# Sixteen of 22 FFN inner tiles from 2x2 block problems, four blocks run into each other, and a key block moved behind a product of the mixer

## The chip, the cores and the metric

One core of a Trainium2 chip runs the whole program: TensorE (PE in the profile), its weight loader (PEld), VectorE (DVE), ScalarE (ACT), GpSimd (POOL) and SyncE (SP), and 16 DMA engines that serve two queues here, a hardware queue fed by SP and a software queue fed by POOL. The metric is the device time of one execution in microseconds, the median of three runs. The kernel before takes 1901.01 us.

## The reference

Two layers, each a token mixer of three branches and a SwiGLU FFN, on 512 rows of 1024 columns, all in float32. What the change touches is the FFN, and in the mixer only an order.

```python
D_MODEL = 1024; SEQ = 512; DEPTH = 2
FFN_HIDDEN = -(-8 * D_MODEL // (3 * 256)) * 256          # 2816, 22 tiles of 128
...
for l in range(DEPTH):
    h = jnp.einsum('bsd,de->bse', x, w_in[l])
    rq, rk, rv, rg, cq, ck, cv, dq, dk, dv, gates = jnp.split(h, splits, axis=-1)
    ...
    x = _layer_norm(DEEPNORM_ALPHA * x + mix, ln1_g[l], ln1_b[l])
    u = jnp.einsum('bsd,df->bsf', x, w_ffn_in[l])
    u_gate, u_up = jnp.split(u, 2, axis=-1)
    ffn = jnp.einsum('bsf,fd->bsd', jax.nn.silu(u_gate) * u_up, w_ffn_out[l])
    x = _layer_norm(DEEPNORM_ALPHA * x + ffn, ln2_g[l], ln2_b[l])
```

## The kernel before

**Arithmetic.** Every float32 operand is held as a pair of float32r values, hi and lo, and a product of two pairs is three matmuls (`mm3`, L122 to L124: hi by hi, lo by hi, hi by lo). A weight block of 128 x 2048 values arrives by DMA in a staging buffer `st` (four of them). ACT casts it to `wh` (L259, or L154 in two pieces of 1024) and DVE subtracts to `wl` (L260, or L155). There are three buffers each of `wh` and `wl`, in rotation: the fourth block from here reuses the buffer of the first, and its cast waits until PE has read that one for the last time. A DVE subtraction waits for the cast of its block.

**Plain tiles.** `u_ffn(i)` makes inner tile i of the FFN: gate and up columns, 8 row blocks, three matmuls each of 128x512, so 48 matmuls into two `pt` banks, then tanh, products and the split into the pair `hid`.

**Block problems.** A 2x2 block problem replaces 8 block products by 7, after Strassen and Winograd. For the FFN's first matrix `u_fin(pb)` makes four inner tiles (gate and up) at once, as seven products called m1, y, m2, v, x, g and h, of 24 matmuls each: 168 matmuls of 128x512 into `pf` banks where four plain tiles take 192. The seven weight operands are sums of four 1 MiB blocks of the matrix. Class `Chain` makes them with four loads by SP (L174) and four accumulating DMAs by POOL (L178, `accum_op=ALU.add`): one staging buffer `a` is loaded for m1, and after each split the next block is added onto it for y, x and h; m2 and v load blocks of their own; g takes a buffer `c` that was filled ahead. An accumulating DMA onto `a` can start only when ACT and DVE have read `a`. Class `Close`, so far used only in the mixer, has five loads and two accumulating DMAs, `a` and `c`, both ahead of their use, and two additions of 128x2048 on DVE (L233, L239) for the other two sums. The seven results are summed on DVE and ACT into natural order (rows by inner columns), where tanh and the products are applied (`gate_half`, `gated`); `s_turn` brings them back by 128x128 transposes on PE into `ph` banks (L1241), eight per call and two calls per block, and ACT copies them out as halves `hf` (L1243).

**Second matrix.** The FFN's output is made in two groups of eight inner tiles by block problems (`fout_items`, o for tiles 0 to 7 and w for 8 to 15, both `Chain`) and a plain rest (tiles 16 to 21, `fout_rest`). The hidden operand of o comes from blocks p and q as `Twins`, whose sums run over halves of 128x512; that of w comes from plain tiles 8 to 15 as `Quarters` (`s_hid`, sums of 128x256 columns, L292 to L295). The first product of o also issues the eight loads of the residual `z` (L455); DVE adds the products to `z` (L1302 the first time, L1304 after).

**Order.** Two lists written by hand, one for the mixer and one for the FFN, give the order of items; an item has its weights, its PE work and two groups of side steps that run within it. Weights are asked for up to three items ahead. A scheduler then moves single instructions of each engine a little. Each engine, SP and POOL work through their instructions strictly in order. In the mixer the two blocks p and q (retention values and gates) are run beside each other's neighbours, and `u_rqk(rk, RK, 1)`, the second key block, stands between q's products m1 and y.

Of the kernel before, what the change touches and what calls it, by code (L numbers as in the profile page):

```python
# [13 lines left out]
F32R = mybir.dt.float32r  # L14
# [14 lines left out]
FFN = 2816  # L29
# [23 lines left out]
REST = 16  # L53
# [3 lines left out]
def trunk(ctx, tc, x_in, xT_in, w_in, ret_norm_g, da_norm_g, lq1, lk1, lq2, lk2, w_a, w_b, w_c, b_merge, w_out,  # L57
# [19 lines left out]
    def g(dt=F32, name="g"):  # L77
        return gp.tile([P, 512], dt, tag="g", name=name)
# [183 lines left out]
    class Quarters:  # L262
# [15 lines left out]

        def parts(self, t1, t2, scale):

            q, p2 = g(F32R, "q11"), Pair("q2")
            part_hi(q[:, self.A], t1[:, self.A], scale)
            part_lo(q[:, self.B], t1[:, self.A], q[:, self.A], scale)
            split(p2, t2, scale=scale)
            self.use["m1"] = q[:, self.A], q[:, self.B]
            self.put("m2", p2, self.A)
            self.put("h", p2, self.B)

        def sums(self, t1, t2, scale=None):
# [12 lines left out]
    class Twins:  # L302
# [33 lines left out]

# [271 lines left out]
    def layer(l):  # L608
# [506 lines left out]
        for (specs, fn), *groups in [  # L1115
# [3 lines left out]
            (p["x"], [q["a"]]), (u_rqk(rq, RQ, 1),), (p["g"], [q["c"]]), (p["h"],),  # L1119
            (q["m1"], [], [s_r2(0)]), (u_rqk(rk, RK, 1), [s_r2(1)], [s_r3(0)]), (q["y"], [], [s_r3(1)]),  # L1120
            (q["v"], [s_dh(2)]), (q["m2"], [], [s_r1(2)]), (q["x"], [s_dh(3)]), (u_cqk(0), [], [s_r1(3)]), (q["g"],), (q["h"],),
            (u_gate(2, 0), [s_r2(2)], [s_r2(3), s_r3(2)]), (u_cqk(1), [s_r3(3)] + c(0)[0], c(0)[1]),
# [72 lines left out]
        def ffn_done(i, pg, pu):  # L1195
            t = g(name="fth")
            nc.scalar.activation(t, pg, AF.Tanh, scale=0.5)
            nc.vector.scalar_tensor_tensor(t, t, 1.0, pg, op0=ALU.add, op1=ALU.mult)
            nc.vector.tensor_mul(t, t, pu)  # L1199
            if i >= REST:  # L1200
                hid[i] = Pair("hid")
                split(hid[i], t, scale=0.5)
            else:
                hid[i] = t

        def s_hid(k):

            def fn():
                r0, kh = GROUPS[1]
                t1, t2 = hid[r0 + k], hid[r0 + kh + k]  # L1210
                hid[r0 + k], hid[r0 + kh + k] = Quarters(), None
                hid[r0 + k].parts(t1, t2, 0.5)
                hid[r0 + k].sums(t1, t2, 0.5)
            return fn

# [31 lines left out]

        def s_ready(fp):
            def fn():
                twins[fp] = Twins(half.pop((0, 0, fp)), half.pop((0, 1, fp)))  # L1250
                twins[fp].ready(half.pop((1, 0, fp)))
                hid[2 * fp], hid[2 * fp + 1] = twins[fp].each
            return fn

        def s_twins(fp):
            def fn():
                twins.pop(fp).sums(half.pop((1, 1, fp)))
            return fn
# [108 lines left out]

        p, q, o, w = u_fin(0), u_fin(1), fout_items(0), fout_items(1)
        for (specs, fn), *groups in [
            (u_ffn_first([8, 9]), [s_natural(0)], [s_x1(0)]), (u_ffn(10), [s_x1(1), s_x1(2)], [s_x1(3), s_natural(1)]),  # L1370
            (p["m1"], [s_natural(2)], [p["c"], s_natural(3)]), (u_ffn(11),), (p["y"],), (p["m2"],),
            (p["v"],), (p["x"],), (u_ffn(12), [], [s_turn(0, 0)]), (p["g"],), (p["h"],),
            (q["m1"], [], [q["c"]]), (u_ffn(13), [s_turn(0, 1)]), (q["y"],), (q["m2"],),
            (q["v"],), (q["x"],), (u_ffn(14), [], [s_turn(1, 0)]), (q["g"],), (q["h"], [s_ready(0)], [s_ready(1)]),
            (o["m1"], [], [s_turn(1, 1)]), (u_ffn(15), [s_twins(0)], [s_twins(1), o["c"]]), (o["m2"],), (o["y"],), (u_ffn(16),),
            (o["v"],), (o["x"],), (u_ffn(17),), (o["g"], [], [s_hid(0)]), (o["h"], [], [s_hid(1)]), (u_ffn(18), [s_hid(2)], [s_hid(3)]),
            (w["m1"],), (u_ffn(19), [], [w["c"]]), (w["m2"],), (w["y"],), (u_ffn(20),),
            (w["v"],), (w["x"],), (u_ffn(21),), (w["g"],), (w["h"],),
        ]:
            item(specs, fn, *groups)  # L1380
# [61 lines left out]
```

## Time and profile before

| | |
|---|---|
| median of three runs | 1901.01 us (1900.52 to 1903.43) |
| profiled execution, its own time | 1905.45 us |
| its span | 1903.7 us, mean granted TensorE clock 0.997 |
| PE busy | 1886.1 us, 99% |
| weight loads (PEld) | 1588.1 us, 83% |
| DVE | 1290.6 us, 68% |
| ACT | 931.2 us, 49% |
| DMA, hardware queue | 237.01 MB, 38.4% of 16 engines' span |
| DMA, software queue (accumulating) | 46.56 MB, 14.5% |

PE is busy nearly all the time, so the time is the length of PE's own work plus the few stretches in which it waits. The recorded duration of a matmul is longer than its pace, because successive matmuls overlap; the pace is read from a stretch of PE time divided by the matmuls in it. The FFN of the first layer lies at 603 to 915 us of the span, that of the second at 1550 to 1861 us. Durations of DVE, ACT and DMA instructions can be read from the groups directly.

### The profile page before, as it was taken

To read this page: it belongs to the slowest core of one execution; us is meant where nothing else is said; L and a number is where in the kernel's file an instruction comes from. 1 tells how busy PE (TensorE), PEld (TensorE's weight loads), DVE (VectorE), ACT (ScalarE), POOL (GpSimd) and SP (SyncE) were. 2 spreads that over 40 slices of the span, in tenths; PEclk is the share of its full clock that TensorE was granted. 3 is DMA by queue.
4 is the path that set the end of the run, shared out by engine and by line. 5 is a ranking of instruction groups with operands and counts; after the bars stand their busy time and mean duration, and the time that the engine had idled before them with its cause. 6 is when DMAs were issued, how large, how long until landed. Compare 5 with 4: busy or idle time off the path is not lost. (4 is left out here: it accounts for less than half of the span.)

```text
span 1903.7 us, 24003 instructions
## 1 busy us (share of the span) xinstructions
PE 1886.1 (99%) x9170; PEld 1588.1 (83%) x9170; DVE 1290.6 (68%) x2047; ACT 931.2 (49%) x1547; POOL 114.0 (6%) x141
## 2 busy tenths in 40 slices
PE   9999999999999999999999999999999999999998
PEld 7888788888888888888898887888888888888886
DVE  6776766667766855775677767566776668467756
ACT  5545555567634444443355545545765344344430
POOL 2000000000000010000010000000000000000000
PEclk9999999999999999999999999999999999999999
DMA  9595344332155577766375844533322546876561
GB/s 282 151 285 150 119 141 128 111 119 81 56 173 160 154 172 179 202 155 155 111 201 171 273 111 122 171 108 109 122 67 77 189 121 165 189 181 185 144 154 44
DMA packets 239346, 285.09 MB, mean 150 GB/s; under 512 B 8580, under 2 KB 147936, under 8 KB 239232
## 3 DMA queue, kind: packets, MB, share of 16 engines
q1 hardware_dynamic: 215232, 237.01, 38.4%
q0 software_dynamic: 24000, 46.56, 14.5%
q8 instruction: 72, 1.18, 0.3%
q14 instruction: 42, 0.34, 0.1%
HBM read 260.42 MB, written 23.12 MB: 149 GB/s over the span
## 5 line engine op out<-in xcount | busy, mean ns | idle before, releaser
L122 PE MATMUL pt<-xTh,wh 128*128 128x512 f32 (+1 forms) x1328 | 498.3, 376 | 0.9 <-ACT wh L154 0.8
L124 PE MATMUL pt<-xTh,wl 128*128 128x512 f32 (+1 forms) x1328 | 494.4, 373 | 0.0
L123 PE MATMUL pt<-xTl,wh 128*128 128x512 f32 (+1 forms) x1328 | 494.3, 372 | 0.0
L155 DVE TENSOR_TENSOR wl<-st,wh 128x1024 fp32r<-128x1024 f32 (+1 forms) x236 | 257.2, 1113 | 102.0 <-ACT wh L154 87.4
L154 ACT CAST wh<-st 128x1024 fp32r<-128x1024 f32 (+1 forms) x236 | 220.2, 961 | 210.8 <-PE pt L123 84.4
L260 DVE TENSOR_TENSOR wl<-st,wh 128x2048 fp32r<-128x2048 f32 x98 | 224.6, 2292 | 122.1 <-ACT wh L259 121.1
L124 PEld LDWEIGHTS pt<-xTh,wl 128*128 128x128 f32 x1328 | 250.6, 189 | 43.9
L122 PEld LDWEIGHTS pt<-xTh,wh 128*128 128x128 f32 x1328 | 250.5, 189 | 43.3 <-ACT wh L154 1.5
L123 PEld LDWEIGHTS pt<-xTl,wh 128*128 128x128 f32 x1328 | 251.1, 189 | 41.8
L259 ACT CAST wh<-st 128x2048 fp32r<-128x2048 f32 x98 | 187.3, 1912 | 173.8 <-PE pt L123 73.9
L122 PE MATMUL pf<-wh,xTh 128*128 128x512 f32 x240 | 94.0, 392 | 0.4 <-ACT rph L106 0.4
L123 PE MATMUL pf<-wl,xTh 128*128 128x512 f32 x240 | 93.9, 391 | 0.0
L124 PE MATMUL pf<-wh,xTl 128*128 128x512 f32 x240 | 93.5, 390 | 0.0
L123 PE MATMUL pf<-wl,s12h 128*128 128x512 f32 x192 | 75.9, 395 | 3.2 <-DVE wl L260 3.2
L122 PE MATMUL pf<-wh,s12h 128*128 128x512 f32 x192 | 75.6, 395 | 2.2 <-ACT wh L259 2.2
L122 PE MATMUL pf<-wh,s43h 128*128 128x512 f32 x192 | 75.8, 395 | 0.0
L124 PE MATMUL pf<-wh,s12l 128*128 128x512 f32 x192 | 75.3, 393 | 0.0
L123 PE MATMUL pf<-wl,s43h 128*128 128x512 f32 x192 | 75.3, 392 | 0.0
L124 PE MATMUL pf<-wh,s43l 128*128 128x512 f32 x192 | 75.1, 391 | 0.0
L383 ACT COPY sw<-pt 32x512 f32<-32x512 f32 (+1 forms) x96 | 55.6, 579 | 33.0 <-PE pt L124 31.8
L1199 DVE TENSOR_TENSOR fth<-fth,pt 128x512 f32<-128x512 f32 x28 | 19.2, 687 | 68.7 <-PE pt L124 68.4
L750 ACT COPY tc<-pf 128x512 f32<-128x512 f32 x60 | 34.1, 586 | 54.2 <-PE pf L124 53.0
(341 smaller groups left out, 3494.4 us busy)
## 6 DMA issues: line engine op xcount, KB each, us to landing
st<-in_w_in SPq DMA_DIRECT2D x60, 1024.0 KB, 5.2
st<-in_w_ffn_in SPq DMA_DIRECT2D x56, 512.0 KB, 5.6
st<-in_w_ffn_out SPq DMA_DIRECT2D x20, 1024.0 KB, 5.1
st<-in_w_in SPq DMA_DIRECT2D x32, 512.0 KB, 5.1
st<-in_w_ffn_in SPq DMA_DIRECT2D x16, 1024.0 KB, 5.8
st<-in_w_ffn_in POOLq DMA_DIRECT2D x16, 1024.0 KB, 9.4
st<-in_w_ffn_out POOLq DMA_DIRECT2D x16, 1024.0 KB, 8.6
st<-in_w_in POOLq DMA_DIRECT2D x12, 1024.0 KB, 11.1
```

The costliest lines, as they stand in the source:

```text
L122: nc.tensor.matmul(ps, lh, rh, start=start, stop=False, skip_group_check=onto)
L123: nc.tensor.matmul(ps, lh, rl, start=False, stop=False, skip_group_check=onto)
L124: nc.tensor.matmul(ps, ll, rh, start=False, stop=stop, skip_group_check=onto)
L154: return [nc.scalar.copy(self.hi[:, a:b], self.st[:, a:b]), nc.vector.tensor_sub(self.lo[:, a:b], self.st[:, a:b], f(self.hi[:, a:b]))]
L155: nc.vector.tensor_sub(self.lo[:, a:b], self.st[:, a:b], f(self.hi[:, a:b]))]
L259: nc.scalar.copy(self.hi, st)
L260: nc.vector.tensor_sub(self.lo, st, f(self.hi))
L383: nc.scalar.copy(sw[half * b:half * b + half], ps[half * o:half * o + half])
L750: nc.scalar.copy(t[to, j], ps)
L1199: nc.vector.tensor_mul(t, t, pu)
```

## The change

In each layer's FFN, inner tiles 0 to 15 come from four block problems p, q, r, u (`Chain`, `Close`, `Chain`, `Close`); six plain tiles, 16 to 21, are left. Both output groups take their hidden operands from halves by `Twins`, whose sums are cut in three (`difference`, `sums`, `rest`) so that each can be placed by itself; `Quarters.parts` and `s_hid` go. A block's m1 stands ahead of the last two products of the block before it, and the first products of the output group o stand inside u. In the mixer's list q's y stands ahead of the second key block instead of behind it.

```diff
         def ready(self, a12):
             self.a12 = a12
             self.part("m1", self.a11)
             self.part("m2", a12)
-        def sums(self, a22):
-            t = g(name="ta")
-            nc.vector.tensor_sub(t, self.a21, a22)
-            self.part("y", t)
+        def difference(self, a22):
+            self.a22, self.t = a22, g(name="ta")
+            nc.vector.tensor_sub(self.t, self.a21, a22)
+            self.part("y", self.t)
+        def sums(self):
+            t = self.t
             nc.vector.tensor_sub(t, t, self.a11)
             self.part("x", t)
             nc.vector.tensor_add(self.a12, self.a12, t)
             self.part("v", self.a12)
+        def rest(self):
             nc.vector.tensor_sub(self.a21, self.a11, self.a21)
             self.part("g", self.a21)
-            self.part("h", a22)
+            self.part("h", self.a22)
...
-            (q["m1"], [], [s_r2(0)]), (u_rqk(rk, RK, 1), [s_r2(1)], [s_r3(0)]), (q["y"], [], [s_r3(1)]),
-            (q["v"], [s_dh(2)]), (q["m2"], [], [s_r1(2)]), ...
+            (q["m1"], [], [s_r2(0)]), (q["y"], [s_r2(1)]), (u_rqk(rk, RK, 1), [], [s_r3(0)]),
+            (q["v"], [s_dh(2)], [s_r3(1)]), (q["m2"], [], [s_r1(2)]), ...
...
-        def u_fin(pb):
-            return u_two(Chain(w_ffn_in[l], 0, 4, (512 * pb, FFN + 512 * pb)), x1q,
+        def u_fin(pb, kind):
+            return u_two(kind(w_ffn_in[l], 0, 4, (512 * pb, FFN + 512 * pb)), x1q,
                          functools.partial(gate_half, pb), functools.partial(gated, pb))
...
-        p, q, o, w = u_fin(0), u_fin(1), fout_items(0), fout_items(1)
+        p, q, r, u = u_fin(0, Chain), u_fin(1, Close), u_fin(2, Chain), u_fin(3, Close)
+        o, w = fout_items(0), fout_items(1)
         for (specs, fn), *groups in [
-            (u_ffn_first([8, 9]), [s_natural(0)], [s_x1(0)]), (u_ffn(10), [s_x1(1), s_x1(2)], [s_x1(3), s_natural(1)]),
-            (p["m1"], [s_natural(2)], [p["c"], s_natural(3)]), (u_ffn(11),), (p["y"],), (p["m2"],),
-            (p["v"],), (p["x"],), (u_ffn(12), [], [s_turn(0, 0)]), (p["g"],), (p["h"],),
-            (q["m1"], [], [q["c"]]), (u_ffn(13), [s_turn(0, 1)]), (q["y"],), (q["m2"],),
-            (q["v"],), (q["x"],), (u_ffn(14), [], [s_turn(1, 0)]), (q["g"],), (q["h"], [s_ready(0)], [s_ready(1)]),
-            (o["m1"], [], [s_turn(1, 1)]), (u_ffn(15), [s_twins(0)], [s_twins(1), o["c"]]), (o["m2"],), (o["y"],), (u_ffn(16),),
-            (o["v"],), (o["x"],), (u_ffn(17),), (o["g"], [], [s_hid(0)]), (o["h"], [], [s_hid(1)]), (u_ffn(18), [s_hid(2)], [s_hid(3)]),
-            (w["m1"],), (u_ffn(19), [], [w["c"]]), (w["m2"],), (w["y"],), (u_ffn(20),),
-            (w["v"],), (w["x"],), (u_ffn(21),), (w["g"],), (w["h"],),
+            (u_ffn_first([16, 17]), [s_natural(0)], [s_x1(0)]), (p["m1"], [s_x1(1)], [s_x1(2)]),
+            (u_ffn(18), [s_x1(3), s_natural(1)], [p["c"]]), (p["m2"], [s_natural(2)], [s_natural(3)]), (p["y"],),
+            (p["v"], [q["a"]]), (u_ffn(19),), (p["x"],), (q["m1"],), (p["g"], [s_turn(0, 0)]), (p["h"],),
+            (q["y"], [q["c"]]), (q["v"], [s_turn(0, 1)]), (q["m2"],), (q["x"],), (r["m1"],), (q["g"], [s_turn(1, 0)]), (q["h"],),
+            (r["y"],), (r["m2"], [s_turn(1, 1)], [r["c"]]), (r["v"], [u["a"]]), (r["x"],), (u["m1"],), (r["g"], [s_turn(2, 0)]),
+            (r["h"], [s_ready(0, 0)], [s_ready(0, 1)]),
+            (u["y"], [u["c"]]), (u["v"], [s_turn(2, 1)]), (u["m2"],), (u["x"],),
+            (o["m1"], [s_differ(0, 0)], [s_differ(0, 1)]), (u["g"], [s_turn(3, 0)]), (u["h"], [s_sums(0, 0)], [s_sums(0, 1)]),
+            (o["m2"],), (o["y"], [s_turn(3, 1)], [o["c"]]), (u_ffn(20), [s_rest(0, 0)], [s_rest(0, 1)]), (o["v"], [s_ready(1, 0)], [s_ready(1, 1)]),
+            (o["x"],), (w["m1"], [s_differ(1, 0)], [s_differ(1, 1)]), (o["g"],), (o["h"], [s_sums(1, 0)], [s_sums(1, 1)]),
+            (w["m2"], [s_rest(1, 0)], [s_rest(1, 1)]), (w["y"], [w["c"]]), (u_ffn(21),), (w["v"],), (w["x"],),
+            (w["g"],), (w["h"],),
```

How this moves instructions is shown at three places of the first layer. The second layer has the same order.

In the mixer, on PE, around q's product x. Before, `wh_1431` is the operand of q's y, `wh_1713` that of q's x, and the two share a buffer; `prt` are transposes of another step.

```order
L122 MATMUL pf_1680<-wh_1431,s12h_616 128x512
L123 MATMUL pf_1680<-wl_1432,s12h_616 128x512
L124 MATMUL pf_1680<-wh_1431,s12l_617 128x512
L853 MATMUL prt_1695<-ident_75,ro_1598 128x128 x2
L853 MATMUL prt_1695<-ident_75,ro_1601 128x128 x2
L853 MATMUL prt_1704<-ident_75,ro_1598 128x128 x2
L853 MATMUL prt_1704<-ident_75,ro_1601 128x128 x2
L122 MATMUL pf_1435<-wh_1713,s12h_472 128x512
```

After, `wh_1695` is the operand of q's x; it shares its buffer with the key block's weights. PE reads those for the last time ahead of eight transposes and the 24 matmuls of q's v (operand `wh_1515`), of which the last three are the first rows here.

```order
L122 MATMUL pf_1583<-wh_1515,s43h_618 128x512
L123 MATMUL pf_1583<-wl_1516,s43h_618 128x512
L124 MATMUL pf_1583<-wh_1515,s43l_619 128x512
L848 MATMUL prt_1729<-ident_75,ro_1577 128x128 x2
L848 MATMUL prt_1729<-ident_75,ro_1580 128x128 x2
L848 MATMUL prt_1738<-ident_75,ro_1577 128x128 x2
L848 MATMUL prt_1738<-ident_75,ro_1580 128x128 x2
L122 MATMUL pf_1435<-wh_1695,s12h_472 128x512
```

Between the last reader of the shared buffer and q's x stood eight transposes; now the whole of v and sixteen transposes stand there.

On POOL, from the last row tiles of the LayerNorm ahead of the FFN (`rs`, a power) to the end of block problems. Before:

```order
L494 TENSOR_TENSOR rs_5331<-rs_5331,mhalf_83 128x1
L494 TENSOR_TENSOR rs_5425<-rs_5425,mhalf_83 128x1
L178 DMA st_5854<-in_w_ffn_in 128x4x512
L178 DMA st_5695<-in_w_ffn_in 128x4x512 x3
L178 DMA st_6248<-in_w_ffn_in 128x4x512
L178 DMA st_6139<-in_w_ffn_in 128x4x512 x3
L178 DMA st_6804<-in_w_ffn_out 128x4x512
L178 DMA st_6541<-in_w_ffn_out 128x4x512 x3
```

After (up to the first accumulation for the second output group):

```order
L489 TENSOR_TENSOR rs_5331<-rs_5331,mhalf_83 128x1
L178 DMA st_5430<-in_w_ffn_in 128x4x512
L489 TENSOR_TENSOR rs_5425<-rs_5425,mhalf_83 128x1
L178 DMA st_5857<-in_w_ffn_in 128x4x512
L178 DMA st_5430<-in_w_ffn_in 128x4x512
L178 DMA st_5970<-in_w_ffn_in 128x4x512
L178 DMA st_5430<-in_w_ffn_in 128x4x512
L178 DMA st_6222<-in_w_ffn_in 128x4x512
L178 DMA st_6286<-in_w_ffn_in 128x4x512
L178 DMA st_6565<-in_w_ffn_in 128x4x512
L178 DMA st_6286<-in_w_ffn_in 128x4x512
L178 DMA st_6588<-in_w_ffn_in 128x4x512
```

The first accumulation now stands ahead of the last `rs`, and accumulations of one block's chain (`st_5430` is p's, `st_6286` is r's) alternate with those for the next block's `a` and `c`.

On DVE, from the first product of o to its second. Before, `wl_6634` and `wl_6696` are splits, the rows L1302 add o's m1 to `z`, and then come the sums of `Twins`.

```order
L260 TENSOR_TENSOR wl_6634<-st_6631,wh_6633 128x2048
L112 TENSOR_TENSOR qm2l_6628<-hf_6539,qm2h_6627 128x512
L260 TENSOR_TENSOR wl_6696<-st_6541,wh_6695 128x2048
L1302 TENSOR_SCALAR z_6637<-z_6637,pf_6653 128x512
L1302 TENSOR_SCALAR z_6639<-z_6639,pf_6667 128x512
L327 TENSOR_TENSOR ta_6754<-hf_6316,hf_6686 128x512
```

After, the same additions (L1295) stand between the last sums of block u and `wl_6992`, the split of o's m2.

```order
L260 TENSOR_TENSOR wl_6930<-st_6770,wh_6929 128x2048
L1211 TENSOR_TENSOR tc12_6854<-fth_6894,tc12_6854 128x512
L1295 TENSOR_SCALAR z_6933<-z_6933,pf_6949 128x512
L1295 TENSOR_SCALAR z_6935<-z_6935,pf_6963 128x512
L317 TENSOR_TENSOR ta_6977<-hf_6263,hf_6539 128x512
L260 TENSOR_TENSOR wl_6992<-st_6989,wh_6991 128x2048
```

The split that PE needs next thus stands behind additions that need the loads of `z`, which on SP come behind the load of that split's own block:

```order
L174 DMA st_6989<-in_w_ffn_out 128x4x512
L450 DMA z_6933<-saved0_80 128x512
L150 DMA st_7092<-in_w_ffn_in 128x8x128
L450 DMA z_6934<-saved0_80 128x512
L450 DMA z_6935<-saved0_80 128x512
L450 DMA z_6936<-saved0_80 128x512
```

Before, the eight loads of `z` (L455) stood in one piece behind the two loads of a plain tile's weights, and the next split behind the additions was that of plain tile 15, not of a product of o.

More of the change, by code (lines that the diff above doesn't have):

```diff
@@ L277, in put @@
             self.use[name] = pr.hi[:, sl], pr.lo[:, sl]
[L279 to L287, printed above, removed]
         def sums(self, t1, t2, scale=None):
@@ L1199, in ffn_done @@
             nc.vector.tensor_mul(t, t, pu)
[L1200 to L1214, printed above, removed]
+            hid[i] = Pair("hid")
+            split(hid[i], t, scale=0.5)
         nat, half = {}, {}
@@ L1246, in layer, with s_ready, s_differ, s_sums @@
         twins = {}
[L1248 removed]
+        def s_ready(gi, fp):
             def fn():
[L1250 to L1252 removed]
+                pa, pc, k = 2 * gi, 2 * gi + 1, 8 * gi + 2 * fp
+                tw = twins[gi, fp] = Twins(half.pop((pa, 0, fp)), half.pop((pa, 1, fp)))
+                tw.ready(half.pop((pc, 0, fp)))
+                hid[k], hid[k + 1] = tw.each
             return fn
[L1255 removed]
+        def s_differ(gi, fp):
             def fn():
[L1257 removed]
+                twins[gi, fp].difference(half.pop((2 * gi + 1, 1, fp)))
+            return fn
+        def s_sums(gi, fp):
+            def fn():
+                twins[gi, fp].sums()
+            return fn
+        def s_rest(gi, fp):
+            def fn():
+                twins.pop((gi, fp)).rest()
             return fn
```

2 lines of the change are left out of this document (1 added, 1 removed).

## The prediction

> **What bounds the kernel now.** I read the head of the profile page first, then the waits of PE, then the FFN in stretches, then the DMA queues.
>
> ```profile
> span 1903.7 us, 24003 instructions
> PE 1886.1 (99%) x9170; PEld 1588.1 (83%) x9170; DVE 1290.6 (68%) x2047; ACT 931.2 (49%) x1547; POOL 114.0 (6%) x141
> ```
>
> ```profile
> PE pf L123 <- DVE wl L260: 3.2, 2, 1.6
> PE pf L122 <- ACT wh L259: 2.2, 2, 1.1
> PE warm L579 <- POOL ident masks.py:199: 1.5, 1, 1.5
> PE pt L122 <- ACT wh L154: 0.8, 1, 0.8
> ```
>
> PE is the bound, and its listed waits (us in total, times, longest) are a few microseconds in the whole program. So a change is worth the PE work it removes, less the waits it makes. Two thirds of the waits are one pair of rows, twice each; the first pair lies here:
>
> ```profile
> PE pf L123 <- DVE wl L260: 1.6, 1, 1.6
> PE pf L122 <- ACT wh L259: 1.1, 1, 1.1
> ```
>
> That is the answer for 190 to 205 us, and it is q's product x in the mixer: its cast waits until y has left the shared buffer, and only eight transposes of PE work cover it. The same pair stands in layer two.
>
> The first layer's FFN, in stretches (columns: length, then busy time and count of PE, PEld, DVE, ACT, POOL, then clock, DMA share, GB/s):
>
> ```profile
> 603.00:915.00 312.00, 311.71 (x1489) 262.12 (x1488) 208.09 (x259) 135.72 (x167) 21.17 (x17) 1.00 0.69 171
> 620.00:660.00 40.00, 40.00 (x211) 34.53 (x211) 36.38 (x54) 17.65 (x21) 2.56 (x2) 1.00 0.59 144
> 740.00:780.00 40.00, 40.00 (x186) 33.10 (x184) 27.46 (x32) 18.53 (x24) 3.88 (x3) 1.00 0.93 236
> 860.00:915.00 55.00, 55.00 (x244) 45.60 (x243) 30.28 (x32) 17.59 (x17) 1.43 (x2) 1.00 0.63 165
> ```
>
> PE idles 0.29 us of 312. DVE has a third free, but only 3.6 of 40 us at the start (620 to 660), and the DMA engines are nearly full at 740 to 780, where four streams meet.
>
> **PE work.** Per layer, eight plain tiles of 48 matmuls go (384) and two blocks of 168 come (336): 48 matmuls of 128x512 fewer, 96 in both layers. Their pace: 860 to 915 holds almost nothing else, so 55.00/244 = 0.225 us, and 96 of them are 21.6 us. Each block brings 16 transposes, 64 in all:
>
> ```profile
> L1241 PE MATMUL ph<-ident,tc x8: 271/272/273, 688.1 to 688.9; 128*128 128x128 f32 x8
> ```
>
> Eight start within 0.8 us, seven steps of some 0.11 us, so 64 x 0.11 = 7.0 us come back. Net −14.6 us. The record of 0.272 us overlaps its neighbours. The Trainium skill ("TensorE: Matmul & The Clock Gate", Part 4: PE-mode transpose) gives about 275 ns for such a transpose within a kernel; the recorded duration agrees, the pace does not. By that figure as a cost the 64 would take 17.6 us and the net would be −4.0; I go by the starts.
>
> **The mixer's order.** With y ahead, x's buffer is the key block's. Between its last reader and x stand 24 matmuls and 16 transposes, 24 x 0.225 + 16 x 0.11 = 7.2 us, against a cast and a subtraction one after the other:
>
> ```profile
> L259 ACT CAST wh<-st 128x2048 fp32r<-128x2048 f32 x98 | 187.3, 1912 | 173.8 <-PE pt L123 73.9
> L260 DVE TENSOR_TENSOR wl<-st,wh 128x2048 fp32r<-128x2048 f32 x98 | 224.6, 2292 | 122.1 <-ACT wh L259 121.1
> ```
>
> 1.9 + 2.3 = 4.2 us, 3.0 to spare. The stall goes whole: 3.2 + 2.2 = −5.4 us. Late next could be y, whose block is accumulated and which now comes a key block (48 matmuls, 10.8 us) earlier:
>
> ```profile
> L178 POOL DMA_DIRECT2D st<-in_w_in x1: 1276/1276/1276, 134.4 to 134.4; - x1
> ...
> DMA to landing us min/median/max: 11.1/11.1/11.1
> ...
> L259 ACT CAST wh<-st x2: 1907/1909/1911, 167.1 to 171.3; 128x2048 fp32r<-128x2048 f32 x2
> ```
>
> It landed at 145.5, and y's cast ran at 167.1; at 156 it still finds its data. At the least, this place gives nothing (0), if the wait moves to another product.
>
> **DVE and ACT.** DVE gains 28 splits and 8 additions of 2048 columns and 44 instructions of 512, and loses 32 of 1024 and 40 of 256:
>
> ```profile
> L155 DVE TENSOR_TENSOR wl<-st,wh 128x1024 fp32r<-128x1024 f32 x27 | 32.3, 1220 | 2.1 <-ACT wh L154 2.1
> L1304 DVE TENSOR_TENSOR z<-z,pf 128x512 f32<-128x512 f32 x19 | 12.9, 684 | 5.5 <-PE pf L124 5.5
> L294 DVE TENSOR_TENSOR sb<-fth,sa 128x256 f32<-128x256 f32 x4 | 1.7, 424 | 0.0
> ```
>
> 36 x 2.29 + 44 x 0.68 − 32 x 1.22 − 40 x 0.42 = +56.5 us, 28 per layer: 208 becomes 236 of about 304 us, 78%. ACT gains 28 x 1.91 less 32 casts of 1024, and stays under half. On average both have room; the cost lies where DVE is already dense. At the start the first tiles' LayerNorm work fills it, and p's m1 and the sums of `Quarters` now come one item earlier: the split of plain tile 19 and the `s12` operands of p's y finish just when PE wants them. Ends: 0, and the missing 1 us if one more 512-column instruction and its wait come ahead; I take 0.3 per layer. On POOL, p's first accumulation, which needs m1's split, now stands ahead of the last LayerNorm power. The power comes some 0.5 us later (estimate: the split's end against the power's operand), but the transposes behind it have moved 1.3 us of PE work later too: 0, between −0.3 and +0.3.
>
> **Transfers.** Per layer SP loads 2 MiB more (20 blocks of 1 MiB in place of 32 halves, both layers) and POOL accumulates 4 MiB more (a `Close` has two, 44 become 52).
>
> ```profile
> q1 hardware_dynamic: 215232, 237.01, 38.4%
> q0 software_dynamic: 24000, 46.56, 14.5%
> st<-in_w_ffn_in SPq DMA_DIRECT2D x16, 1024.0 KB, 5.8
> st<-in_w_ffn_in POOLq DMA_DIRECT2D x16, 1024.0 KB, 9.4
> ```
>
> Queue time per MiB: 0.384 x 1903.7/226.0 = 3.2 us plain, 0.145 x 1903.7/44.4 = 6.2 us accumulating. So 2 x 3.2 + 4 x 6.2 = 31 us more in an FFN that has 0.69 x 312 = 215: 246 of 304, 81%. Off the path where spread, but blocks r and u without a plain tile between them ask for five accumulations and six loads, 31 + 19 = 50 us of transfers, within about 49 us of PE work (nine products of 24 x 0.225 = 5.4 us). How full engines and a queue behind another accumulation bear on a landing:
>
> ```profile
> L178 POOL DMA_DIRECT2D st<-in_w_ffn_out x3: 1282/1282/1435, 831.4 to 858.9; - x3
> ...
> DMA to landing us min/median/max: 8.4/8.6/13.7
> ```
>
> Alone 8.4 to 8.6, right behind another 13.7: 5 us later. Products x and h of r each need such an accumulation that starts after the split before and stands behind one for u. By PE work between, x has about a microsecond less than 13.7 + 1.9, h two to three less in the bad case. Ends per layer: 0 (as at 740 to 780, 93% full and PE without a wait) and 4; I take 2.
>
> **The residual.** PE's second product of o needs `wl_6992`, behind two additions to `z`. Loads of `z` are 256 KB each, one behind another on SP, which has to wait there for a free buffer that `qm1h_6738` of o's first operand reads:
>
> ```profile
> L455 SPq DMA_DIRECT2D z<-saved x8: 319/379/2673, 761.1 to 767.5; - x8
> ...
> DMA to landing us min/median/max: 4.9/5.4/7.0
> ...
> L1302 DVE SCALAR_TENSOR_TENSOR z<-z,pf x8: 681/682/687, 771.4 to 834.0; 128x512 f32<-128x512 f32 x8
> ```
>
> Before, issue to first addition took 10 us, with plain tile 15 behind it as cover (10.8 us of PE work). Now only u's g and h cover it. Landing of the third load 5 to 7 us after its issue, then an addition (0.68), a difference (0.68), a split (2.29): PE waits 0.2 us at 4.9 and about 3 us at 7 plus one load ahead in the queue. I take 1.5 per layer. The last place is o's g, behind w's m1, whose operand's cast on ACT comes 0.5 us early to 1.5 us late: 0.6 per layer.
>
> **Sum.** New waits 0.3 + 2 + 1.5 + 0.6 = 4.4 per layer, 8.8 in all. Against the profiled execution: 1905.45 − 14.6 − 5.4 + 8.8 = 1894.2. That execution lies 4.4 us above the median of 1901.01, so 1889.8, forecast 1890.
>
> **Rivals.**
> 1. *No new wait.* Speaks for it: 740 to 780 at 93% DMA without a wait. 1901.0 − 20.0 = 1881.
> 2. *Accumulations in one file.* POOL's queue is strict, so a `Chain` accumulation late by some microseconds also holds back the `Close` ones behind it, and each product of r, u, o and w waits in turn. Ten to twelve products per layer lie behind such landings; at 1 us each it is 10 to 12 per layer, and 24 us eat the gain and 4 us more: 1901 − 20 + 24 = 1905. It decides from about 1 us mean lateness. Against it: a late product also gives the next transfers time. The Trainium skill ("SBUF — State Buffer", section "SBUF: two separate sides") describes a way there: while DVE holds the shared port, GpSimd cannot write the descriptors of its DMAs. By that rule a busier DVE makes accumulations later. The trace here: accumulations took 8.5 to 9.4 us at 603 to 660, where DVE is fullest, and 8.4 to 8.7 at 860 to 915 where it is at 55%.
>
> ```profile
> DMA to landing us min/median/max: 8.5/9.4/9.4
> ...
> DMA to landing us min/median/max: 8.4/8.5/8.7
> ```
>
> Under 1 us apart, so the cost of that mechanism is small here.
> 3. *The mixer's stall only moves.* 1890 + 5.4 = 1895.
> 4. *DVE late in o and w.* At 36.38 of 40 us it kept up, at over 40 it cannot; the sums of `Twins`, the additions to `z` and splits meet in o: 10 us over both layers, 1900.
>
> **How the numbers follow.** This kernel's runs tell about 0.2% (3.8 us) from no change: 1897.2 and 1904.8 are the bounds. Forecast (1885 to 1896) 0.50; rival 1 (1879 to 1885) 0.19; rival 3 (1892 to 1898) 0.08; rival 4 (1896 to 1902) 0.13; rival 2 (above 1902) 0.10. Range 1880 to 1900, from no wait at all to twice the waits I priced. Faster: 0.50 + 0.19 + 0.07 of rival 3 and 0.03 of rival 4 = 0.79; same 0.01 + 0.10 + 0.02 of rivals 3, 4 and 2 = 0.13; slower 0.08, all of rival 2.
>
> **What would show it.** PE busy down by about 15 us; no row for a wait on L259 and L260 near 190 us; PE waits on `pf` matmuls behind ACT casts of accumulated blocks in r and behind `wl` in o's m2, of 1 to 3 us; DVE near 78% of the FFN and the DMA share near 0.8. Wrong would be: waits of some microseconds at each product from r on, or a row for DVE at 40 of 40 us.

## The result and the profile after

The changed kernel takes 1892.53 us (median of four runs, 1891.41 to 1893.32), the kernel before 1902.22 us beside it: a ratio of 0.9946 with a 95% interval of 0.9930 to 0.9962, some 7 to 13 us. The forecast was 1890, its range 1880 to 1900. So the time is right; the parts of which it is made are less so, as the experiments show.

The head of the page of the changed kernel, and its DMA queues:

```profile
span 1889.6 us, 24024 instructions
PE 1869.7 (99%) x9138; PEld 1573.4 (83%) x9138; DVE 1344.3 (71%) x2055; ACT 973.5 (52%) x1579; POOL 124.4 (7%) x149
q1 hardware_dynamic: 192512, 241.20, 38.4%
q0 software_dynamic: 28224, 54.95, 17.1%
```

The waits of PE in the changed kernel (us in total, times, longest):

```profile
PE pf L122 <- DVE tc L760: 4.9, 2, 2.5
PE pt L123 <- DVE xTl L112: 1.9, 2, 1.0
PE warm L574 <- POOL ident masks.py:199: 1.5, 1, 1.5
PE pf L123 <- DVE wl L260: 1.2, 2, 0.7
PE pf L122 <- ACT rph L106: 0.8, 2, 0.4
PE pf L122 <- DVE z L1297: 0.5, 2, 0.2
```

The rows of L259 and L260 from the mixer are gone (the L260 row left is o's m2). In their place stands a wait of nearly the same size, 2.4 to 2.5 us per layer, behind DVE's L760. PE adds the products of a block into banks of PSUM, its accumulation memory. L760 reads the bank that holds r's g (it subtracts it from a sum `tc`), and PE may add r's h onto that bank only after the read. Around it, in the first layer (length, busy time and count of PE, PEld, DVE, ACT, POOL, granted clock, DMA share, GB/s):

```profile
603.00:907.00 304.00, 300.64 (x1429) 251.69 (x1430) 229.06 (x257) 151.24 (x175) 26.29 (x21) 0.99 0.76 191
762.00:767.00 5.00, 2.57 (x13) 1.82 (x11) 4.51 (x4) 4.65 (x5) 0.00 (x0) 1.00 0.49 142
767.00:771.00 4.00, 4.00 (x11) 3.17 (x12) 2.60 (x2) 0.00 (x0) 1.28 (x1) 0.57 0.23 87
```

The wait lies in the second row. The third is what I had not reckoned with: PE is busy for all of the 4 us, but it gets through 11 matmuls instead of 18 or so, at a granted clock of 0.57. That is 4 x 0.43 = 1.7 us on top of the wait. The drop itself is 3.4 us long, from 767.3 us, at a clock of exactly 0.50; the last section shows what sets it off.

Why L760 is late is seen on POOL. Its two accumulations that were issued between 740 and 750 us, first the one for block u, then the one for r's h (in the section on the change POOL's list ends at the first of the two, `st_6588`; r's h and u's `c` come next):

```profile
L178 POOL DMA_DIRECT2D st<-in_w_ffn_in x2: 1292/1573/1854, 743.4 to 744.1; - x2
...
  ACT wh L259: 8.4, 1
busy tenths in 40 slices 0000000000000000000000000000000000000000
DMA to landing us min/median/max: 8.9/11.9/15.0
```

The second is issued 0.7 us behind the first and lands 15.0 us after its issue, at 759. ACT's next cast had waited 8.4 us for it, and everything behind that cast in ACT's queue with it. DVE's queue shows the rest (start, length, instruction, in brackets the idle time before it and what ended that):

```profile
761.13 2.29 DVE L260 TENSOR_TENSOR wl<-st,wh 128x2048 fp32r<-128x2048 f32 x1 [5.40 <-ACT wh L259]
763.91 2.29 DVE L260 TENSOR_TENSOR wl<-st,wh 128x2048 fp32r<-128x2048 f32 x1 [0.49 <-ACT wh L259]
766.12 1.28 DVE L760 TENSOR_TENSOR tc<-tc,pf 128x512 f32<-128x512 f32 x2
```

DVE stands idle for 5.4 us until that cast is done. Then the split of this block and the split of the next run one behind the other from 761.1 to 766.2 us, and L760 stands behind both. So a late transfer shows up as a wait for a subtraction two steps on.

### The profile page after: what moved, and what is told of

Its sections match the earlier page's. It is cut to its first block, busy times and chain, and to the rows that moved or that the text cites. A ratio compares the mean times of both kernels' runs of the same rounds, so it can differ in the third digit from the quotient of the medians.

```text
span 1889.6 us, 24024 instructions
## 1 busy us (share of the span) xinstructions
PE 1869.7 (99%) x9138; PEld 1573.4 (83%) x9138; DVE 1344.3 (71%) x2055; ACT 973.5 (52%) x1579; POOL 124.4 (7%) x149
## 5 line engine op out<-in xcount | busy, mean ns | idle before, releaser
L122 PE MATMUL pt<-xTh,wh 128*128 128x512 f32 (+1 forms) x1072 | 397.2, 372 | 0.4 <-ACT wh L154 0.4
L123 PE MATMUL pt<-xTl,wh 128*128 128x512 f32 (+1 forms) x1072 | 393.5, 367 | 1.9 <-DVE xTl L112 1.9
L124 PE MATMUL pt<-xTh,wl 128*128 128x512 f32 (+1 forms) x1072 | 393.6, 368 | 0.0
L260 DVE TENSOR_TENSOR wl<-st,wh 128x2048 fp32r<-128x2048 f32 x126 | 288.3, 2289 | 143.5 <-ACT wh L259 143.3
L259 ACT CAST wh<-st 128x2048 fp32r<-128x2048 f32 x126 | 241.1, 1913 | 181.5 <-PE pf L124 91.1
L123 PEld LDWEIGHTS pt<-xTl,wh 128*128 128x128 f32 x1072 | 202.3, 189 | 34.1 <-DVE xTl L112 2.3
L124 PEld LDWEIGHTS pt<-xTh,wl 128*128 128x128 f32 x1072 | 202.0, 188 | 33.7
L122 PEld LDWEIGHTS pt<-xTh,wh 128*128 128x128 f32 x1072 | 202.0, 189 | 33.0 <-ACT wh L154 1.0
L122 PEld LDWEIGHTS pf<-wh,xTh 128*128 128x128 f32 x336 | 63.5, 189 | 21.6 <-ACT wh L259 5.7
L124 PEld LDWEIGHTS pf<-wh,xTl 128*128 128x128 f32 x336 | 63.5, 189 | 13.3
## 6 DMA issues: line engine op xcount, KB each, us to landing
st<-in_w_in POOLq DMA_DIRECT2D x12, 1024.0 KB, 10.9
```

Of the source, the lines that this page charges most:

```text
L122: nc.tensor.matmul(ps, lh, rh, start=start, stop=False, skip_group_check=onto)
L123: nc.tensor.matmul(ps, lh, rl, start=False, stop=False, skip_group_check=onto)
L124: nc.tensor.matmul(ps, ll, rh, start=False, stop=stop, skip_group_check=onto)
L259: nc.scalar.copy(self.hi, st)
L260: nc.vector.tensor_sub(self.lo, st, f(self.hi))
```

## The experiments

The theory: the time is PE's work plus a few waits; the mixer's stall goes, and the new wait in r comes from the place of one accumulation behind another. The rivals: the stall only moves; the new wait comes from DVE having too much to do, or from full DMA engines, whatever the order. All kernels of one group ran on the same chip, the first four beside a kernel before of 1903.53 us, the next four of 1903.84, the last four of 1903.91.

**The change again.**

> The changed kernel as it is, for comparison on the same chip: 1892.5 us, ratio 0.9946 to the kernel before. Both theories alike.

1893.22 us (1889.11 to 1894.42), ratio 0.9945 (0.9933 to 0.9957). In this execution both waits in r had slow matmuls behind them:

```profile
768.00:774.00 6.00, 5.80 (x14) 4.58 (x15) 2.86 (x3) 0.30 (x1) 1.28 (x1) 0.50 0.42 102
1709.00:1713.00 4.00, 3.60 (x9) 2.94 (x10) 3.06 (x3) 0.10 (x1) 1.28 (x1) 0.57 0.38 148
```

**The mixer's part alone.**

```diff
--- kernel before
-            (q["m1"], [], [s_r2(0)]), (u_rqk(rk, RK, 1), [s_r2(1)], [s_r3(0)]), (q["y"], [], [s_r3(1)]),
-            (q["v"], [s_dh(2)]), ...
+            (q["m1"], [], [s_r2(0)]), (q["y"], [s_r2(1)]), (u_rqk(rk, RK, 1), [], [s_r3(0)]),
+            (q["v"], [s_dh(2)], [s_r3(1)]), ...
```

> The kernel before with the mixer's part of the change alone (q's y ahead of the second key block). Theory: the two pairs of waits on L259 and L260, 5.4 us in all, are gone and no new one takes their place, so 1902.2 - 5.4 = 1896.8 us, ratio 0.997. Rival (the stall only moves to another product): a wait of 2 us or more on another pf matmul in each layer, and a time within 1 us of before.

1895.04 us (1894.85 to 1895.55), ratio 0.9958 (0.9944 to 0.9971). The stall does not move; the largest waits that are left:

```profile
PE warm L579 <- POOL ident masks.py:199: 1.5, 1, 1.5
PE pt L122 <- ACT wh L154: 1.1, 1, 1.1
PE pf L122 <- ACT rph L106: 0.8, 2, 0.4
PE px L505 <- DVE z L496: 0.5, 2, 0.3
```

By the medians it is worth 8.5 us (interval 5.5 to 10.7), more than the 5.4 us of the waits. The trace of the kernel before has the rest, at the same stall in the second layer:

```profile
1143.90:1150.70 6.80, 6.08 (x14) 4.79 (x15) 3.90 (x6) 2.15 (x5) 0.00 (x0) 0.50 0.60 195
```

The clock is halved for 6.8 us, 3.4 us lost. In the first layer's stall, of the same length, the clock stayed at 1.00. So in that execution the two stalls cost about 5.4 + 3.4 = 8.8 us.

**Without u's accumulation.**

```diff
     # class Close, ahead_a
             self.a = self.load(0, 0)
-            self.more(self.a, 0, 1)
+            if self.cols != (512 * 3, FFN + 512 * 3):
+                self.more(self.a, 0, 1)
```

> The changed kernel without one accumulating DMA per layer, the one that makes block u's first operand a (so u's y is computed with an unsummed block). Theory: the 2.4 us wait in front of r's h (recorded as PE behind DVE tc L760) comes from r's accumulation for h, which stands behind u's on POOL's queue and lands after 15 us instead of 9; ACT's queue waits for it, and the splits behind it push the additions that free PE's bank. Without u's accumulation it lands after 8.5 to 9.5 us, both waits of 2.4 and 2.5 us are gone, 4.9 us less than the changed kernel: 1887.6 us. Rival (DVE has too many splits ahead of those additions, whatever the transfers do): the two waits stay at 2 us or more, and the time within 1 us of 1892.5.

1884.32 us (1883.29 to 1884.56), 8.9 below the change. The accumulation for r's h is now alone:

```profile
L178 POOL DMA_DIRECT2D st<-in_w_ffn_in x1: 1292/1292/1292, 744.5 to 744.5; - x1
...
DMA to landing us min/median/max: 8.9/8.9/8.9
```

It landed 8.9 us after its issue, both waits behind the subtraction are gone, and no stretch at a lower clock follows. DVE's queue is the same as in the changed kernel there, so DVE having too much to do is ruled out as the cause by itself. The 8.9 us are more than the 4.9 us that were expected, because the half clock behind the waits went too, 5.1 us of it in the traced execution of the changed kernel beside this one. The run leaves out a transfer as well as its place ahead of r's; the run that changes the order alone comes below.

**p's m1 one item later.**

```diff
-            (..., [s_natural(0)], [s_x1(0)]), (p["m1"], [s_x1(1)], [s_x1(2)]),
-            (u_ffn(18), [s_x1(3), s_natural(1)], [p["c"]]),
+            (..., [s_natural(0)], [s_x1(0)]), (u_ffn(18), [s_x1(1)], [s_x1(2)]),
+            (p["m1"], [s_x1(3), s_natural(1)], [p["c"]]),
```

> The changed kernel with plain tile 18 ahead of p's m1, so that p's 2048-column split comes one item later. Theory: the wait of 0.96 us at the FFN's start (PE behind DVE xTl L112) comes from that split of 2.29 us standing in DVE's queue ahead of the last xTl; with the two splits of 1024 in its place it falls to 0.3 us or less, some 1.3 us less in both layers: 1891.2 us. Rival (POOL's queue: p's accumulation ahead of the last power): the power moves ahead again here too, so the trace must show by the queue which of the two ended last; the time is the same as by the theory. Rival (DVE is just as full one item later): the wait moves to p's second product and the time stays within 0.5 us of 1892.5.

1893.73 us (1891.68 to 1894.88), no gain that can be told. The wait at the FFN's start fell from 0.96 to 0.3 us as expected, but in this execution the two waits in r measured 6.0 us instead of 4.9 to 5.3, which takes back about half of the 1.3 us, and the median is no lower than the changed kernel's. In the changed kernel's trace p's split runs on DVE from 600.3 to 602.6 us, the next `xTl` behind it until 602.9, and PE goes on at 603.0; the power on POOL runs only after that, at 603.7. So the split is what PE waited for there, not POOL's queue, though this run, which moves both, does not part them.

**r's accumulation ahead of u's.** As many accumulations as in the change, in another order:

```diff
+    class Shared(Close):
+        def m1(self):
+            self.a = self.load(0, 0)
+            b = self.block(self.a)
+            self.more(self.a, 0, 1)
+            return b
...
-        p, q, r, u = u_fin(0, Chain), u_fin(1, Close), u_fin(2, Chain), u_fin(3, Close)
+        p, q, r, u = u_fin(0, Chain), u_fin(1, Close), u_fin(2, Chain), u_fin(3, Shared)
...
-            ... (r["v"], [u["a"]]), ...
+            ... (r["v"],), ...
```

> The changed kernel with block u's first operand made as in Chain: m1 and y share one staging buffer, so u's accumulation starts after u's m1 is split and stands behind r's last one on POOL's queue (before: ahead of it); as many accumulations as in the changed kernel, one plain load fewer per layer, DVE's order the same. Theory (the order on POOL's queue makes the wait): r's accumulation for h lands after some 9 us instead of 15, the waits of 2.2 to 3.0 us behind the additions of L760 are gone, and with them the stretches at half the granted clock that followed them; some 7 us below the changed kernel's 1893.2 and within 2 us of the run without u's accumulation (1884.3). Rival (the DMA engines are simply full there): r's accumulation still takes 12 us or more and a wait of 1.5 us or more stays in each layer; time 1889 or more.

1885.97 us (1884.76 to 1886.39), ratio 0.9908 (0.9896 to 0.9921): 7.2 us below the change and 17.9 below the kernel before, with nothing of the computation left out. The one accumulation issued at 740 to 750 us is now r's, and u's follows at 751.2 us:

```profile
L178 POOL DMA_DIRECT2D st<-in_w_ffn_in x1: 1292/1292/1292, 744.9 to 744.9; - x1
...
DMA to landing us min/median/max: 8.8/8.8/8.8
```

A wait behind the same subtraction (L768 in this kernel) stays, 0.9 and 0.7 us, and the clock holds in the 4 us after it:

```profile
PE pf L122 <- DVE tc L768: 1.6, 2, 0.9
```

```profile
764.00:768.00 4.00, 3.13 (x15) 2.27 (x14) 3.34 (x4) 1.91 (x1) 1.28 (x1) 1.00 0.14 50
768.00:772.00 4.00, 4.00 (x19) 3.32 (x18) 3.74 (x3) 1.79 (x3) 0.00 (x0) 1.00 0.96 137
```

So it was the place on POOL's queue, not the number of accumulations. The traces show the same in another way: of two accumulations issued within a microsecond the first lands as if it were alone (8.9 us in the changed kernel) and only the second is late, so the second is served behind the first. The run takes one plain load out as well, and u's accumulation starts some 8 us later than in the change; over 744 to 759 us the DMA share is 0.83 for 0.98. These are not parted from the order.

**A plain tile between r and u.**

```diff
-            ... (r["v"], [u["a"]]), (r["x"],), (u["m1"],), ...
+            ... (r["v"], [u["a"]]), (r["x"],), (u_ffn(20),), (u["m1"],), ...
-            (u_ffn(20), [s_rest(0, 0)], [s_rest(0, 1)]), (o["v"], [s_ready(1, 0)], [s_ready(1, 1)]),
+            (o["v"], [s_rest(0, 0), s_rest(0, 1)], [s_ready(1, 0), s_ready(1, 1)]),
```

> The changed kernel with plain tile 20 moved from behind o's y to between r's x and u's m1 (10.9 us of PE work that need no accumulation). Theory: r's accumulation, 15 us late or not, is covered; the two waits in front of r's h are gone, 4 to 8 us less, unless o, now without a plain tile, waits in their place. Rival (order or load somewhere else): the wait moves to o's v or g, 2 us or more per layer, and the time stays within 2 us of 1893.2.

1906.60 us (1904.10 to 1913.55), ratio 1.0018 (1.0007 to 1.0028): the rival is right that the waits move to o, but the time is 13.4 us above the changed kernel's, where it had at most 2. L760 is gone from the list of waits; in its place in r stand waits of 1.6 and 1.8 us for a split. And o, without the tile, now waits twice in a row, and the clock falls there:

```profile
PE pf L123 <- DVE wl L260: 2.8, 2, 2.5
PE ph L1223 <- DVE fth L1211: 2.2, 1, 2.2
```

```profile
815.00:835.00 20.00, 20.00 (x93) 16.55 (x93) 17.85 (x20) 9.06 (x10) 2.59 (x2) 1.00 1.07 309
835.00:850.00 15.00, 10.27 (x39) 7.79 (x38) 12.39 (x15) 5.85 (x10) 2.56 (x2) 0.77 0.76 167
```

(The first two rows are PE's waits at 800 to 860 us, the others the stretches there.) DVE is busy 17.85 of 20 us ahead of it and the DMA engines are full; PE is idle 4.7 of 15 us. It is the place that the fourth rival of the prediction names, and dearer than its price. That DVE alone is late there is not shown: with tile 20 in its place the changed kernel has DVE busy 18.62 of 20 us at 815 to 835 and waits of only 0.7 and 0.2 us at 800 to 860, and in this run DVE sits idle for 2.3 us ahead of the first of them, behind ACT, whose queue had waited 2.6 us for an accumulation. Against the changed kernel's second execution PE waits 6.5 us more in the whole program and loses 5.1 us more to half clock, 11.6 of the 12.1 us between the two.

**All four blocks as Chain.**

```diff
-        p, q, r, u = u_fin(0, Chain), u_fin(1, Close), u_fin(2, Chain), u_fin(3, Close)
+        p, q, r, u = u_fin(0, Chain), u_fin(1, Chain), u_fin(2, Chain), u_fin(3, Chain)
...     # and without q["a"], u["a"]
```

> The changed kernel with all four FFN blocks as Chain: 4 more accumulations (24 instead of 20 per layer in the FFN), 2 plain loads and 4 additions on DVE fewer per layer. By the rival of the prediction that accumulations in one file decide, each of q's and u's products waits about 1 us or more: over 1900 us. By the theory (only an accumulation that stands behind another is late) q and u run as p and r do, with no wait over 1 us where no two meet: 1884 to 1890 us.

1910.62 us (1906.53 to 1912.80), ratio 1.0038 (1.0025 to 1.0051): slower than before, as the second rival of the prediction had it, but by another route. The theory's 1884 to 1890 us is missed by over 20, since its condition did not hold: three pairs of accumulations per layer are issued within a microsecond, for two in the changed kernel, and the second of each lands after 16.0 to 18.1 us. It is not a mean lateness of a microsecond at each product either; a few waits are long. POOL's at 765 to 772 us, and PE's waits at 760 to 795:

```profile
L178 POOL DMA_DIRECT2D st<-in_w_ffn_in x2: 1282/1563/1844, 768.1 to 768.8; - x2
...
DMA to landing us min/median/max: 9.0/13.2/17.4
```

```profile
PE pf L122 <- ACT tc L745: 5.5, 1, 5.5
PE pf L122 <- DVE tc L760: 3.1, 1, 3.1
```

**Three waits taken away.** The kernel with the shared buffer, p's m1 later as above, and

```diff
-                    if name == "m1" and gi == 0:      # in o's m1
-                        load_res(saved[2 * l])
...
-            ... (u["x"],),
+            ... (u["x"], [s_res]),                    # s_res: load_res and x2["fresh"]
```

> The kernel of the first run here (u's m1 and y share a buffer) with two more waits taken away: p's m1 behind plain tile 18, and the residual's loads issued one item earlier, in u's x. Theory: the waits of 0.96 us at the FFN's start, and those of 0.2 to 0.7 us in o's m2, go too, 2 to 3 us below that kernel: about 1882 us. Rival: with the last of the larger waits gone they are taken up by the next wait behind them; within 1 us of that kernel.

1885.51 us (1884.72 to 1887.16): within 0.5 us of the kernel with the shared buffer alone. The rival's bound fits. Of the two further waits only the one at the FFN's start shrank, from 1.9 to 0.5 us; the 0.2 us in o's m2 stayed, others grew, and all of PE's listed waits together fell only from 7.3 to 6.9 us.

**A measured wait, small and large.**

```diff
                 c = t.pop(("c22", j))
+                if j == 0 and hv.cols == (1024, FFN + 1024):
+                    junk = g(name="junk")
+                    for _ in range(1):                # 6 in the other
+                        nc.vector.tensor_copy(junk, ps)
                 nc.vector.tensor_sub(c, c, ps)
```

> The kernel with u's m1 and y in one buffer (1886.0 us; waits of 0.9 and 0.7 us in front of r's h) with one extra DVE copy of 128x512 per layer in front of the subtraction that PE waits for there: each of the two waits becomes about 0.7 us longer, 1.4 to 1.6 us. Theory (a wait costs itself, and beyond some 2 us also a stretch at half clock behind it): no stretch of slow matmuls behind it, 1886.0 + 1.4 = 1887.4 us, all runs within 1 to 2 us of each other. Rival (any wait of over a microsecond lowers the clock): slow stretches as behind waits of 2.2 to 3.0 us, 1889 us or more.

> The same with six such copies per layer: each of the two waits some 4.1 us longer, 4.5 to 5 us. Theory: 8.2 us of wait and behind each wait a stretch at half the granted clock worth 1.5 to 3 us, 1886.0 + 8.2 + 3 to 6 = 1897 to 1900 us. Rival (the wait costs no more than itself): 1894.2 us and no stretch of matmuls at half pace.

With one copy 1886.36 us (1885.24 to 1887.76), 0.4 above. The waits there did not grow (1.3 us in both layers together; the instructions around moved), so this run says nothing on the clock. With six copies, 1895.57 us (1895.17 to 1897.26), 9.6 above. The wait did not grow to one of 4 to 5 us either but broke into three (PE's waits at 760 to 790 us, then the stretches):

```profile
PE pf L123 <- DVE wl L268: 1.8, 1, 1.8
PE ph L1235 <- DVE fth L1223: 0.9, 1, 0.9
PE pf L122 <- DVE tc L772: 0.8, 1, 0.8
```

```profile
776.00:781.00 5.00, 3.22 (x14) 2.08 (x12) 3.30 (x4) 4.35 (x5) 0.00 (x0) 1.00 0.65 213
781.00:786.00 5.00, 4.07 (x11) 3.21 (x12) 5.00 (x6) 1.88 (x3) 0.00 (x0) 0.66 0.00 0
```

The waits of 0.9 and 1.8 us that follow each other closely are followed by 5 us at a clock of 0.66 in the first layer, and by 6 us at 0.72 in the second: 5 x 0.34 = 1.7 us lost in each. Waits grew by 4.8 us in both layers together (6.6 against 1.8 in these rows), so 8.2 of the 9.6 us are accounted for. It supports the theory that a wait costs more than itself, not the sizes I gave.

**The mixer's part undone in the changed kernel.**

```diff
+            (q["m1"], [], [s_r2(0)]), (u_rqk(rk, RK, 1), [s_r2(1)], [s_r3(0)]), (q["y"], [], [s_r3(1)]),
-            (q["m1"], [], [s_r2(0)]), (q["y"], [s_r2(1)]), (u_rqk(rk, RK, 1), [], [s_r3(0)]),
...     # and s_r3(1) back from q's v to q's y
```

> The changed kernel with the mixer's part undone (the second key block ahead of q's y again). Theory: what the mixer's part brings does not depend on the FFN: its two pairs of waits come back (5.4 us) and a stretch at lower clock in some of them, 5.4 to 8.5 us above the changed kernel's 1893.2, 1898.6 to 1901.7 us. Rival (the two parts overlap, a wait in the one hides one in the other): less than 4 us above it.

1901.36 us (1898.52 to 1902.87), ratio to the kernel before 0.9984 (0.9975 to 0.9993). Each run against the kernel before beside it, the FFN's part alone is worth 2.5 us, the mixer's alone 8.5 and both 10.3. So the mixer's part is worth 7.8 us on top of the FFN's, and within the spread of the runs the two parts add up.

**Transposes twice.**

```diff
-                    for i in range(2):
+                    for i in (0, 1, 0, 1):
                         for j in range(2):
                             o, c = 256 * i + P * j, P * (2 * fp + i)
```

> The kernel with u's m1 and y in one buffer with each of the 128 transposes of the hidden tiles made twice (the second writes the same values again): 128 more. By the pace of the starts, 0.11 us each: 14 us more, 1900 us. By the recorded duration taken as a cost, 0.27 us each: 35 us more, 1921 us.

1896.91 us (1896.70 to 1897.70): 10.9 us for 128 transposes, 0.085 us each, and PE busy 1881.2 instead of 1867.7 us, 0.105 each. The waits behind the subtraction are gone in it, which hides 1.6 us of the cost and accounts for most of the difference between the two. The pace holds, the recorded duration is no cost.

## Why the prediction was right, point by point

| term | forecast, both layers | measured | from |
|---|---|---|---|
| PE work | −14.6 | −13.5 | PE busy 1880.5 (mixer's part alone) to 1867.0 (without u's accumulation), two traces at a mean clock of 0.999 |
| mixer's stall | −5.4 | −8.5, −7.8 | alone; undone; both with the half clock behind it |
| FFN's start | +0.6 | +1.3 | 1.9 against 0.6 before |
| transfers in r and u | +4.0 | +4.9, and slow matmuls | waits behind L760 |
| o's m2 | +3.0 | +1.2 | L260 row |
| o's g | +1.2 | +0.5 | L1297 row |
| half clock behind new waits | none | +1.7, +5.1 | two executions of the changed kernel |
| sum | −11.2 | −9.7, −10.3 | medians of two groups |

**PE work.** Right, 1.1 us too much. The pace of the transposes, 0.11 us forecast, measured 0.085 to 0.105 us. The Trainium skill ("TensorE: Matmul & The Clock Gate", Part 4: PE-mode transpose) gives about 275 ns for a 128x128 bf16 transpose within a kernel: the recorded duration of these float32 ones, 272 ns, agrees, the cost does not.

**The mixer's order.** The mechanism was right: the shared buffer, the stall gone whole, y not late. The step that was mis-sized is "The stall goes whole: 3.2 + 2.2 = −5.4 us". The waits were 5.4 us; the stall cost some 8, because of the half clock behind it (3.4 us in the traced execution).

**New waits.** All four places named did wait, and their sum of 8.8 us met 7.9 (1.3 + 4.9 + 1.2 + 0.5). That h of r "stands behind one for u" was right, and r's h is where PE waited; that PE would wait for its operand was wrong, it waited for the bank. For x the reading was wrong: x's accumulation (724.0 us) stands behind the one for r's own `c` (723.2 us). It landed 15.1 us after its issue, and PE did not wait for x. What was left out here is again a price: no term for what follows a wait.

**Why the time came out.** The same omission stands on both sides. The stall that went and the wait that came are of one size, 2.7 and 2.4 us per layer, and both are followed by slow matmuls in some of the layers. So the two errors nearly cancel, and that they did is luck: which waits the half clock follows differs from execution to execution. Between the two profiled executions (1905.45 and 1891.41 us, 14.0 less) the terms are −13.5 of PE work, −5.4 and −3.4 for the stalls and their half clock, +7.9 and +1.7 for the new waits and theirs, −12.7 in all; 1.3 us stay open.

**The rivals.** No new wait (1881): not so; with r's accumulation put first the time comes within 5 us of it, 1886. Accumulations in one file: not in this change; four more per layer give that rival's time (1910.6 for 1905), but by a few long waits and not by one at each product. A busier DVE did not make accumulations later in general: with DVE at 75% of the FFN instead of 67% their median landing was 9.0 us, against 9.4 and 8.6 before. The stall only moves: no. DVE late in o: not in this change; without plain tile 20 the waits do stand there, with DVE's part in them not shown alone. DVE reached 229 of 304 us, 75%, for 78 forecast, and the DMA share 0.76 for 0.81.

## What to carry to other kernels

Where one engine is 99% busy, count the work first, then each wait. Where one wait, or several close together, leave PE idle for 1.8 us or more out of some 3.4, put another 1.7 us or 3.4 us on it for the clock. Look for two accumulating transfers that are issued within a microsecond of each other: in these traces the second lands 5 to 9 us later than one alone, and the order in the queue decides whose consumer pays. A wait for an addition or a bank can be a late transfer two queues back; follow it by what ACT and DVE were waiting for before.

## What the runs showed of the hardware

**The clock behind a wait.** Right behind single PE waits of 0.96 us or less no trace here shows a stretch of slow matmuls, the program's start left out. After the waits of 2.2 to 3.0 us in r the clock of the next 4 to 6 us was 0.50 to 0.57 in three of the four cases of the two executions of the changed kernel, and 1.00 in the fourth. What decides it can be read from the traces. The clock is either 1.00 or 0.50, and a stretch at 0.50 lasts 3.413 us, or two or three times that (the program's end left out). Within one execution such stretches begin whole multiples of 3.413 us apart: in the second traced execution of the changed kernel at 767.2, 1709.3 and 1886.7 us, 276 and 328 steps from the first. So each execution has a fixed grid of 3.4 us. Here are steps of that grid at the stalls of the kernel before and at the waits of the changed one; PE's idle time is the length less its busy time, the first two columns:

```profile
195.00:198.40 3.40, 2.29 (x14) 1.53 (x12) 3.14 (x3) 2.60 (x3) 0.00 (x0) 1.00 0.00 0
198.40:201.80 3.40, 1.81 (x8) 1.42 (x8) 3.40 (x4) 3.12 (x6) 0.00 (x0) 1.00 0.16 25
201.80:205.20 3.40, 3.40 (x16) 2.82 (x15) 1.47 (x3) 0.02 (x1) 0.00 (x0) 1.00 1.04 359
1140.50:1143.90 3.40, 1.41 (x9) 0.73 (x7) 3.14 (x3) 3.40 (x5) 0.00 (x0) 1.00 0.00 0
1143.90:1147.30 3.40, 2.68 (x6) 2.15 (x7) 3.40 (x6) 2.15 (x5) 0.00 (x0) 0.50 0.45 133
```

```profile
763.90:767.30 3.40, 0.97 (x5) 0.52 (x4) 3.39 (x3) 2.75 (x3) 0.00 (x0) 1.00 0.80 240
767.30:770.70 3.40, 3.40 (x10) 2.66 (x9) 2.30 (x2) 0.00 (x0) 1.28 (x1) 0.50 0.18 68
1702.60:1706.00 3.40, 2.58 (x12) 1.80 (x10) 2.92 (x2) 3.40 (x5) 0.00 (x0) 1.00 0.35 77
1706.00:1709.40 3.40, 1.70 (x8) 1.42 (x8) 3.40 (x4) 1.40 (x1) 0.00 (x0) 1.00 0.79 290
1709.40:1712.80 3.40, 3.40 (x16) 2.82 (x15) 2.38 (x3) 1.11 (x2) 1.28 (x1) 1.00 0.26 17
```

The stall of 2.7 us in the first layer fell into two steps, 1.1 and 1.6 us idle, and the clock held; in the second layer 2.0 us of it fell into one step, and the next was at half clock. It is the same with the two waits in r: 2.4 us in one step halved the clock of the next, 0.8 and 1.7 us in two did not. Over all traces, the program's start left out, each of the 16 steps at full clock with 1.82 us or more of idle PE was followed by one at half clock, and none with 1.75 us or less. So what counts here is idle time of more than about half of one step, by one wait or by several, and a wait's place on the grid, which differs from execution to execution. The rule is read from these traces; no run was made to test it.

The Trainium skill ("TensorE: Matmul & The Clock Gate", Part 1: The HAM clock gate) puts the drop after an idle window of about 3.4 us, and says that this window runs free of the program. The traces agree with half the clock, with the 3.4 us and with a window that runs free; they differ in how much idle time it takes, 1.82 us of it.

That the waits and this half clock make the time can be checked run by run. In the 11 profiled executions of kernels with the changed kernel's PE work the span goes from 1882.4 to 1906.3 us. Less PE's waits (6.5 to 23.4 us) and less half of the time at half clock (0 to 10.2 us, the program's end left out) 1875.7 to 1878.7 us are left. It fits that the runs of a kernel without waits long enough for the drop lie within 0.7 to 2.5 us of each other, and those of a kernel with them within 2 to 9 us.

**Pairs of accumulations.** In the FFN one alone mostly lands 8.4 to 9.4 us after its issue. Of two issued within a microsecond (38 pairs in all traces) the first lands after 8.4 to 10.8 us and the second after 13.8 to 18.1 us. The kernel before showed it at 13.7 us, for two issued 1.2 us apart. A late second costs nothing where its product is far enough off: the pair at 723.2 and 724.0 us in the changed kernel brings PE no wait.
